# A softmax-times-V kernel: the first bank's normalisation of the last head in a pass placed behind its last transposed copy, that head's exponentials taken row by row, and the last loads cut as 3, 2, 1, 1, 1 rows

## The chip, the cores and the metric

The kernel runs on one core of a Trainium2 chip. The metric is the device time of one execution in microseconds. The kernel before took 1064.57 us (median of 3 runs, 1064.5 to 1064.79). Times in traces are counted from the start of the profiled span, which is some 2 us shorter than the time of the same run.

## The reference

```python
# scores: 8 x 12 x 1024 x 1024 float32, v: 8 x 12 x 1024 x 64 float32
scores_max = np.max(scores, axis=-1, keepdims=True)
attn = np.exp(scores - scores_max)
attn = attn / (np.sum(attn, axis=-1, keepdims=True) + 1e-8)
return np.matmul(attn, v).astype(np.float32)
```

There are 96 heads. The scores alone are 403 MB, read once, so this is a kernel of transfers.

## The kernel before

One pass of a hardware loop works off four heads (k = 0 to 3); there are 24 passes. A head has 8 "rows" (tiles of 128 x 1024). A row goes through these stations: a load by DMA; ScalarE's exponential into fp16; eight transposes on TensorE into a PSUM tile `psT`; VectorE's copy of that into `pt`; eight products with V on TensorE, two rows later in program order. A column of ones beside V gives the sum of the exponentials. After the product of row 3 the first PSUM bank of an odd head is complete, after row 7 the second; `normalise` takes the reciprocal of the sums and multiplies (one reciprocal, two products on VectorE for each bank). No maximum is subtracted.

```python
    def finish(u):                      # the products of one row
        ...
        for c in range(C):
            nc.tensor.matmul(out=bank[:, g * M : (g + 1) * M],
                lhsT=pt[:, c * P : (c + 1) * P], rhs=st["vones"][:, c, 0:M], ...)
        if k % 2 == 1:
            if g == G - 1:
                normalise(k, st, b, b + 1)          # b: bank 0 or 1
        elif r == R - 1:
            normalise(k, st, 0, R // G)
        ...
    # in last(n0), behind the last pass but one: the loads of the very last head, in parts of rows
                load(AHEAD - 1, BH - 1, (2,))
                store(n0, AHEAD - T)
                load(AHEAD - 1, BH - 1, (2, 2, 1, 1), 2)
        ...
    def heads(n0):
        for k in range(AHEAD):
            for r in range(R):
                if r % EB == 0:                      # EB = 2 rows an exponential
                    p_nat = take(p_bufs)
                    rows = 1 if k == AHEAD - 1 and r == R - EB else EB
                    for g in range(0, EB, rows):
                        nc.scalar.activation(...)
                for c in range(C):
                    nc.tensor.transpose(...)
                pt = take(pt_bufs)
                nc.vector.tensor_copy(out=pt[:], in_=psT[:])
                ...
                if len(pending) > LAG:               # LAG = 2
                    finish(pending.pop(0))
```

(Cuts are marked by dots.)

The softmax here doesn't subtract the row's maximum and nothing guards it: scores larger than these inputs give would overflow.

## Time and profile before

| | before |
|---|---|
| time, median of 3 runs | 1064.57 us |
| profiled span | 1062.5 us |
| bytes moved | 453 MB |
| last row of scores landed | 1052.02 us |
| last copy on VectorE starts | 1055.87 us |
| VectorE's last product ends | 1058.37 us |
| last store landed | 1060.67 us |

The prediction below shows the slices and the tail. From the page's list of queues and its table of costly groups, only these lines are added (queue: packets, MB, share of the time of 16 engines; group: line, engine, operation, count, busy us, mean ns, idle before):

```profile
q1 hardware_dynamic: 25056, 453.00, 99.3%
...
L253 ACT ACTIVATE p_nat<-s_nat 128x2048 f16<-128x2048 f32 (+1 forms) x408 | 704.9, 1800 | 219.3 <-DMA s_nat<-in_scores_dram 192.2
```

The queue is full for 99.3% of the span, and the busiest compute engine spends most of its idle time waiting for loaded scores. As long as a change to the engines doesn't move the loads, it can only show after the last byte has landed.

### The profile page before, as it was taken

What the parts mean: (1) busy time and instruction counts of PE and PEld (TensorE: products, weight loads), DVE (VectorE), ACT (ScalarE), POOL (GpSimd) and SP (SyncE); (2) the same over time, 40 slices, a digit from 0 to 9 for tenths busy, and PEclk for the clock granted to TensorE, in tenths of its full rate; (3) what the DMA queues carried; (4) which work ended last, traced back from release to release, by engine and by line L of the source; (5) the groups of instructions that cost most, each with busy time, mean ns of one, the idle gap of its engine ahead of it and who ended that gap; (6) DMA issues with size and microseconds to landing.
All of it is one profiled execution on the core that took longest, in us unless ns stands there. A gap on an engine that the chain in (4) does not pass through costs nothing.

```text
span 1062.5 us, 32878 instructions
## 1 busy us (share of the span) xinstructions
PE 722.2 (68%) x12288; PEld 679.8 (64%) x12288; DVE 682.4 (64%) x1205; ACT 735.7 (69%) x432; POOL 243.5 (23%) x406
## 2 busy tenths in 40 slices
PE   2766766667766767666676666767667676667676
PEld 2765766657666667666676656757666576666675
DVE  1766666757566666666676656766667566666667
ACT  3766776666767668576675866767666677666686
POOL 3123212131121311212112221122121311203113
PEclk9888888888789798887888988888888988887989
DMA  9999999999999999999999999999999999999996
GB/s 398 429 418 434 429 434 434 432 435 432 431 429 432 430 432 435 434 433 432 435 424 434 433 429 435 427 441 433 432 432 427 433 429 435 434 433 433 432 427 257
DMA packets 25060, 453.06 MB, mean 426 GB/s; under 512 B 2784, under 2 KB 2784, under 8 KB 9312
## 3 DMA queue, kind: packets, MB, share of 16 engines
q1 hardware_dynamic: 25056, 453.00, 99.3%
q8 instruction: 4, 0.07, 0.0%
HBM read 436.21 MB, written 25.17 MB: 434 GB/s over the span
## 4 chain that ended last, share of the span: by engine, by line
DMA 61%; PE 15%; PEld 5%; ACT 5%; DVE 4%; issue 3%; POOL 3%; SPq 1%; POOLq 1%; ACTq 0%; PEldq 0%
DMA s_nat<-in_scores_dram 61%; PE psT L265 8%; PE psO L144 6%; ACT p_nat L253 5%; DVE pt L271 4%; PEld L265 3%; POOL vones L210 3%; PEld L144 2%; PE psO_whole L144 2%; SPq L201 1%; SPq L189 0%; POOLq L210 0%; POOLq L227 0%; POOLq L288 0%; POOLq L316 0%
## 5 line engine op out<-in xcount | busy, mean ns | idle before, releaser
L253 ACT ACTIVATE p_nat<-s_nat 128x2048 f16<-128x2048 f32 (+1 forms) x408 | 704.9, 1800 | 219.3 <-DMA s_nat<-in_scores_dram 192.2
L265 PE MATMUL psT<-order,p_nat 128*128 128x128 f16 x6144 | 565.0, 247 | 262.6 <-ACT p_nat L253 261.7
L271 DVE COPY pt<-psT 128x1024 f16<-128x1024 f16 x768 | 519.5, 690 | 348.4 <-PE L144 126.7
L265 PEld LDWEIGHTS <-p_nat 128*128 128x128 f16 x6144 | 448.6, 124 | 284.2 <-ACT p_nat L253 281.8
L210 POOL CAST vones<-v_sb 32x512 f16<-32x512 f32 x400 | 242.8, 607 | 815.9 <-PE L265 315.9
L144 PEld LDWEIGHTS <-pt 128*128 128x128 f16 x6144 | 303.9, 107 | 92.9 <-DVE pt L271 89.2
L144 PE MATMUL psO<-vones,pt 128*128 128x65 f16 x3072 | 183.2, 202 | 59.9 <-DVE pt L271 59.6
L144 PE MATMUL psO_whole<-vones,pt 128*128 128x65 f16 x3072 | 189.3, 209 | 12.3 <-DVE pt L271 11.9
L253 ACT ACT_TABLE_LOAD x24 | 30.8, 1283 | 98.5 <-DMA s_nat<-in_scores_dram 81.7
L128 DVE TENSOR_TENSOR out_sb<-psO,recip 64x256 f32<-64x256 f32 x192 | 81.2, 423 | 6.0
L128 DVE TENSOR_TENSOR out_sb<-psO_whole,recip 64x512 f32<-64x512 f32 x96 | 66.0, 688 | 3.1
L123 DVE RECIPROCAL recip<-psO 128x4 f32<-128x4 f32 x96 | 17.0, 177 | 17.2 <-PE psO L144 17.2
L123 DVE RECIPROCAL recip<-psO_whole 128x8 f32<-128x8 f32 x48 | 9.5, 198 | 0.0
L71 DVE MEMSET vones<- 128x16 f16 x4 | 0.2, 72 | 0.8 <-PEq L305 0.8
L62 DVE CAST order<-ident 128x128 f16<-128x128 f32 x1 | 0.2, 227 | 0.4 <-POOL ident masks.py:199 0.4
masks.py:199 POOL TENSOR_SCALAR_AFFINE_SELECT ident<-ident 128x128 f32<-128x128 f32 x1 | 0.3, 292 | 0.1
masks.py:197 POOL MEMSET ident<- 128x128 f32 x1 | 0.2, 204 | 0.3 <-POOLq L305 0.3
L305 POOL MEMSET const-float32-0.0<- 128x1 f32 x1 | 0.1, 98 | 0.3 <-issue 0.3
L305 POOL MEMSET const-bfloat16-1.0<- 128x1 bf16 x1 | 0.1, 100 | 0.0
L305 POOL MEMSET const-uint8-127<- 128x1 uint8 x1 | 0.1, 100 | 0.0
L305 POOL MEMSET const-float32-1.0<- 128x1 f32 x1 | 0.1, 98 | 0.0
## 6 DMA issues: line engine op xcount, KB each, us to landing
s_nat<-in_scores_dram SPq DMA_DIRECT2D x96, 4096.0 KB, 32.2
v_sb<-in_v_dram SPq DMA_DIRECT2D x24, 1024.0 KB, 18.4
out_dram<-out_sb SPq DMA_DIRECT2D x47, 512.0 KB, 27.6
s_nat<-in_scores_dram SPq DMA_DIRECT2D x2, 2048.0 KB, 33.4
s_nat<-in_scores_dram SPq DMA_DIRECT2D x3, 1024.0 KB, 27.4
s_nat<-in_scores_dram SPq DMA_DIRECT2D x2, 512.0 KB, 20.7
out_dram<-out_sb SPq DMA_DIRECT2D x2, 256.0 KB, 2.0
```

Of the source, the lines that this page charges most:

```text
L62: nc.vector.tensor_copy(out=order16[:].rearrange("p (t j) -> p t j", t=T), in_=ident32[:].rearrange("p (j t) -> p t j", t=T),)
L71: nc.vector.memset(vo[:, :, D : D + 2], 1.0)
L123: nc.vector.reciprocal(out=recip, in_=psO[:, :, :, D : D + 1])
L128: nc.vector.tensor_tensor(out=rows.rearrange("j (b g) d -> j b g d", g=G), in0=psO[part, :, :, 0:D], in1=recip[part].to_broadcast([W, last ...
L144: nc.tensor.matmul(out=bank[:, g * M : (g + 1) * M], lhsT=pt[:, c * P : (c + 1) * P], rhs=st["vones"][:, c, 0:M], start=(c == 0), stop=(c ...
L201: nc.sync.dma_start(out=v_sb[:].rearrange("x h s l d -> x (h s l d)"), in_=rows[bass.ds(n // AHEAD, 1)].rearrange("o x y -> (o x) y"),)
L210: nc.gpsimd.tensor_copy(out=vones_bufs[k][s * Q : (s + 1) * Q, :, 0:D].rearrange("i (h l) d -> i h l d", l=L), in_=v_sb[k * Q : (k + 1) * ...
L253: nc.scalar.activation(out=p_nat[:, g : g + rows, :].rearrange("p r (x v) -> p x r v", v=Q * L), in_=s_bufs[k][:, r + g : r + g + rows, :] ...
L265: nc.tensor.transpose(out=psT[:, c * P : (c + 1) * P], in_=p_row[:, c // L, c % L, :], identity=order16[:],)
L271: nc.vector.tensor_copy(out=pt[:], in_=psT[:])
L305: nc = _bacc.Bacc("TRN2", target_bir_lowering=False, num_devices=1)
```

## The change

The intent: the first bank's reciprocal and products of the last head stand on VectorE in front of the last copy, on which everything after it depends. They are ordered behind that copy, where VectorE otherwise waits for the last products. And the last head comes in smaller parts behind a first one of three rows, with an exponential for each single row, so that ScalarE need not wait for a pair. The order on VectorE and the single-row exponentials (from row 2 on) apply to the last head (k = 3) of every pass, the parts of the loads to the very last head alone.

```diff
-    def normalise(k, st, first, last):
+    def normalise(k, st, first, last, behind=None):
...
-        nc.vector.reciprocal(out=recip, in_=psO[:, :, :, D : D + 1])
+        inverse = nc.vector.reciprocal(out=recip, in_=psO[:, :, :, D : D + 1])
+        if behind is not None:
+            after(inverse, behind)
...
-            if g == G - 1:
+            if g == G - 1 and (b > 0 or k < AHEAD - 1):
                 normalise(k, st, b, b + 1)
...
-                load(AHEAD - 1, BH - 1, (2,))
+                load(AHEAD - 1, BH - 1, (3,))
                 store(n0, AHEAD - T)
-                load(AHEAD - 1, BH - 1, (2, 2, 1, 1), 2)
+                load(AHEAD - 1, BH - 1, (2, 1, 1, 1), 3)
...
-                    rows = 1 if k == AHEAD - 1 and r == R - EB else EB
+                    rows = 1 if k == AHEAD - 1 and r > 0 else EB
...
-                nc.vector.tensor_copy(out=pt[:], in_=psT[:])
+                copy = nc.vector.tensor_copy(out=pt[:], in_=psT[:])
+                if k == AHEAD - 1 and r == R - 1:
+                    normalise(k, st, 0, 1, copy)
```

## The prediction

> **What bounds the kernel now.** I read the page's slices first, then the last 40 us engine by engine in order of time, then single semaphore updates.
>
> The 40 slices of the page:
>
> ```profile
> DMA  9999999999999999999999999999999999999996
> GB/s 398 429 418 434 429 434 434 432 435 432 431 429 432 430 432 435 434 433 432 435 424 434 433 429 435 427 441 433 432 432 427 433 429 435 434 433 433 432 427 257
> ```
>
> For 39 slices the DMA engines are full at about 430 GB/s; only the last slice (26.6 us wide) is not. The change leaves the bytes (453 MB) alone. What it does in the first 23 passes lies beside a full transfer queue (loads take some 32 us from issue to landing, so three are always queued), so I count it as zero, and only the tail can pay.
>
> VectorE in order of time, from 1049.2 us to the end (start, length, operation, idle before it):
>
> ```profile
> 1049.26 0.69 DVE L271 COPY pt<-psT 128x1024 f16<-128x1024 f16 x1 [0.21 <-PE L144]
> 1049.87 0.20 DVE L123 RECIPROCAL recip<-psO_whole 128x8 f32<-128x8 f32 x1
> 1050.10 1.41 DVE L128 TENSOR_TENSOR out_sb<-psO_whole,recip 64x512 f32<-64x512 f32 x2
> 1051.54 2.48 DVE L271 COPY pt<-psT 128x1024 f16<-128x1024 f16 x4
> 1053.94 0.18 DVE L123 RECIPROCAL recip<-psO 128x4 f32<-128x4 f32 x1
> 1054.24 0.69 DVE L271 COPY pt<-psT 128x1024 f16<-128x1024 f16 x1
> 1054.96 0.88 DVE L128 TENSOR_TENSOR out_sb<-psO,recip 64x256 f32<-64x256 f32 x2
> 1055.87 0.69 DVE L271 COPY pt<-psT 128x1024 f16<-128x1024 f16 x1
> 1057.28 0.18 DVE L123 RECIPROCAL recip<-psO 128x4 f32<-128x4 f32 x1 [0.72 <-PE psO L144]
> 1057.49 0.88 DVE L128 TENSOR_TENSOR out_sb<-psO,recip 64x256 f32<-64x256 f32 x2
> ```
>
> Counted back from the end: the copy at 1055.87 is row 7 of the last head, 1054.24 row 6, the four at 1051.54 rows 2 to 5, 1049.26 row 1. Reciprocal and products at 1053.94 to 1055.84 normalise the first bank (rows 0 to 3); nothing needs them until the final store, yet they stand in front of the last copy, on which the last product on TensorE and all after it depend. After that copy VectorE idles 0.72 us.
>
> It looks as if VectorE, busy without a break, were the bound. It is not, quite. TensorE and VectorE in order of time while the first head of this pass is worked off (one fence each):
>
> ```profile
> 1028.57 0.61 PE L265 MATMUL psT<-order,p_nat 128*128 128x128 f16 x8
> 1029.28 0.62 PE L265 MATMUL psT<-order,p_nat 128*128 128x128 f16 x8
> 1029.99 0.61 PE L265 MATMUL psT<-order,p_nat 128*128 128x128 f16 x8
> ```
>
> ```profile
> 1029.73 0.69 DVE L271 COPY pt<-psT 128x1024 f16<-128x1024 f16 x1 [0.27 <-PE L144]
> 1030.69 0.69 DVE L271 COPY pt<-psT 128x1024 f16<-128x1024 f16 x1 [0.27 <-PE L144]
> 1031.65 0.69 DVE L271 COPY pt<-psT 128x1024 f16<-128x1024 f16 x1 [0.27 <-PE psO_whole L144]
> ```
>
> The transposes of rows 5, 6, 7 start 0.71 us apart, their copies 0.96 us apart, each after 0.27 us of idle VectorE, the last one over a microsecond after its transposes seem done. The trace records every semaphore update, and there the answer is: TensorE's semaphore rises by one for each of the 32 instructions of a row (8 weight loads and 8 matmuls for the transposes, as many for the product), one every 0.030 us, so 0.96 us a row, and each of these copies starts within 0.01 us of the update that completes its own transposes. In the tail these updates run without a break from before 1049.27 (row 1's transposes counted) to 1051.64, pause until 1051.88, and run on: row 5 at 1053.29, row 6 at 1054.24, row 7 at 1055.20. Row 6's copy (1054.24) waits for that; row 7's (1055.87) does not, it is 0.67 us late because of the first bank's products.
>
> ScalarE in the same stretch:
>
> ```profile
> 1047.23 1.92 ACT L253 ACTIVATE p_nat<-s_nat 128x2048 f16<-128x2048 f32 x1 [0.67 <-PE L144]
> 1049.64 3.81 ACT L253 ACTIVATE p_nat<-s_nat 128x2048 f16<-128x2048 f32 x3 [0.49 <-PE L265]
> ```
>
> Its two waits are put down to TensorE, but the loads' semaphores show rows 2 and 3 landing at 1047.13, rows 4 and 5 at 1049.54, row 6 at 1050.77, row 7 at 1052.02: it waits for data. The exponentials of rows 4 and 5 end at 1051.56, their transposes start at 1051.61, and that is the pause in the updates.
>
> [...] the last store here is issued from SyncE, and takes 2.05 us from issue at 1058.62 to landing at 1060.67. Nothing in the change shortens that.
>
> **The change, part by part.** Nothing is removed; one normalisation moves, ScalarE gets two more instructions a pass, the last loads are cut otherwise.
>
> *Loads 3,2,1,1,1.* A row of 0.5 MB takes 1.2 us (1049.54, 1050.77, 1052.02). By that step rows 0 to 2 land at 1043.38 + 1.2 = 1044.6, then the store, rows 3 and 4 at 1048.35; rows 5, 6, 7 stay at 1049.54, 1050.77, 1052.02. Total and last landing are the same.
>
> *Single-row exponentials.* A single row takes 1.04 us alone and 0.95 from start to start, against 1.80 for a back-to-back pair: 0.1 us more for a pair, twice a pass, on an engine busy 69%. In the tail row 2 ends near 1047.6, row 3 at 1049.5, row 4 at 1050.45 (1.1 us sooner than now), row 5 at 1051.4, row 6 at 1052.35, row 7 at 1053.3 (now 1053.45). So TensorE no longer pauses for row 4. Counting 0.03 us an instruction on from 1049.27 without the pause, in the changed kernel's own order, 192 instructions bring row 7's transposes to 1049.27 + 5.76 = 1055.03: 0.17 us sooner.
>
> *The moved normalisation.* VectorE's order also changes nearby: row 2's copy now stands before the two large products of the head before. From 1050.07: row 2 waits for its transposes at 1050.23 and ends at 1050.92; large products to 1052.36; row 3 to 1053.08; rows 4, 5 and 6 at 0.60 us steps to 1053.69, 1054.28 and 1054.89 (row 6's transposes are counted at 1054.07); row 7 can start at 1054.81, so its transposes decide: 1055.04 to 1055.73, against 1055.87 to 1056.56 now. The first bank then takes reciprocal and products, 1055.65 to 1056.75. The last product on TensorE is counted 16 instructions after row 6's at 1055.99, at 1056.47 (or 0.69 us after the copy, as now: 1056.42), inside that time, so the 0.72 us wait vanishes and VectorE goes on: second bank 1056.78 to 1057.88, against 1058.37 now. The store follows each half as now. **Sum: 0.49 us**, of which 0.17 from the pause and some 0.32 from the move. 1064.57 - 0.49 = 1064.08.
>
> **The rivals.**
> 1. VectorE's instructions are the bound. Then taking 1.13 us of first-bank work (with its gap) from before the last copy brings that copy forward by all of it, and with the first bank filling the idle 0.72 us the end comes 0.8 us sooner: 1063.8. For it: no idle over 0.2 us before 1056.56. Against: rows 6 and 7 are ready by the count only at 1054.07 and 1055.03.
> 2. The extra 0.27 us returns. Rows 6 and 7 now follow a copy directly, with the two-wait form of instruction that shows 0.27 us of idle elsewhere. If that form itself cost 0.27 us, row 7 would end near 1056.2 and nothing would be gained: 1064.5. Against: the same form without idle at row 6 of the second head (start 1038.70, the count at 1038.71).
> 3. Last landing or TensorE's final product takes over: row 7 lands at 1052.02 and is needed near 1054.5, about 1.2 us spare after its exponential; the product has 0.3 us spare. A slip there costs tenths: 1064.3.
> 4. GpSimd's four casts after the last product run to 1060.02 now, the store's landing to 1060.67; both move earlier, so the casts stay hidden. No effect.
> 5. The first 23 passes gain or lose through earlier stores: with DMA at 99.3% I expect nothing. Were I wrong by 0.05 us a pass, that would be 1.2 us.
>
> **Range and chances.** The mechanisms span 0.0 to 0.8 us; the three runs of before spread over 0.3 us, and another session may shift the level by some tenths. So 1064.1, from 1063.4 to 1064.7. Two per cent is 21 us, more than the whole unfilled tail after the last landing (10.5 us): within 2% at 0.98, 0.01 on either side for a slow execution.
>
> **What would show it.** In the changed profile the last copy starts at the count of its transposes, near 1055.0 relative to the same loads, with no idle of 0.7 us behind it; two reciprocals and four products follow each other to VectorE's end, near 1057.9; no TensorE pause before row 4. Wrong, if the last copy starts well before the count would allow (rival 1), if 0.27 us gaps stand before rows 6 and 7 with the count long done (rival 2), or if the slices before the last change their GB/s (rival 5).

(0.49 us is 0.17 from the pause and some 0.32 from the move, all from the times and the 0.030 us steps read above.)

## The result, and the profile after

The changed kernel took **1064.06 us** (median of 6 runs, 1063.72 to 1064.94); the kernel before took 1064.59 us in the same rounds (6 runs, 1064.39 to 1064.93). A ratio here is the mean time of one kernel's fast runs over the mean of the other's of the same rounds, so not quite the ratio of the medians: it is 0.9996, with a 95% interval from 0.9984 to 1.0009. By the times alone this is "the same"; that there is a real half microsecond must come from the traces, and from the fact that the difference of the medians was 0.53, 0.66 and 0.47 us in three sets of rounds.

The slices of the page after:

```profile
DMA  9999999999999999999999999999999999999996
GB/s 397 430 417 434 428 434 434 432 435 428 434 432 432 427 433 435 434 434 427 433 429 435 428 433 435 426 441 431 431 434 429 430 428 438 434 434 432 426 432 260
```

The first 39 slices are as full as before: the first 23 passes gained and lost nothing.

VectorE of the changed kernel in order of time (start, length, operation, idle before it):

```profile
1049.42 0.69 DVE L273 COPY pt<-psT 128x1024 f16<-128x1024 f16 x1 [0.21 <-PE L146]
1050.03 0.20 DVE L123 RECIPROCAL recip<-psO_whole 128x8 f32<-128x8 f32 x1
1050.38 0.69 DVE L273 COPY pt<-psT 128x1024 f16<-128x1024 f16 x1 [0.15 <-PE L146]
1051.11 1.41 DVE L130 TENSOR_TENSOR out_sb<-psO_whole,recip 64x512 f32<-64x512 f32 x2
1052.54 2.48 DVE L273 COPY pt<-psT 128x1024 f16<-128x1024 f16 x4
1055.18 0.69 DVE L273 COPY pt<-psT 128x1024 f16<-128x1024 f16 x1 [0.16 <-PE L146]
1055.79 0.17 DVE L123 RECIPROCAL recip<-psO 128x4 f32<-128x4 f32 x1
1056.00 0.88 DVE L130 TENSOR_TENSOR out_sb<-psO,recip 64x256 f32<-64x256 f32 x2
1056.91 0.18 DVE L123 RECIPROCAL recip<-psO 128x4 f32<-128x4 f32 x1
1057.12 0.88 DVE L130 TENSOR_TENSOR out_sb<-psO,recip 64x256 f32<-64x256 f32 x2
```

Row 7's copy starts at 1055.18, the trace's record of TensorE's semaphore completes that row's transposes at 1055.16, and the idle of 0.16 us in front of it is that wait. Behind it two reciprocals and four products follow without the idle of 0.72 us of before. Row 2's copy now stands before the two large products, as the prediction said.

ScalarE of the changed kernel:

```profile
1048.45 4.86 ACT L255 ACTIVATE p_nat<-s_nat 128x1024 f16<-128x1024 f32 x5 [0.93 <-PE L267]
```

Five single rows in one unbroken run, the last one ending at 1053.30 (before 1053.45). Rows 3 and 4 landed at 1048.37; here too the wait is put down to TensorE, where the landing was last.

TensorE's transposes and VectorE's copies while the second half of this pass's first head is worked off (one fence each), as in the prediction:

```profile
1029.15 0.61 PE L267 MATMUL psT<-order,p_nat 128*128 128x128 f16 x8
...
1029.85 0.61 PE L267 MATMUL psT<-order,p_nat 128*128 128x128 f16 x8
...
1030.56 0.61 PE L267 MATMUL psT<-order,p_nat 128*128 128x128 f16 x8
```

```profile
1030.01 0.69 DVE L273 COPY pt<-psT 128x1024 f16<-128x1024 f16 x1 [0.27 <-PE L267]
1030.97 0.69 DVE L273 COPY pt<-psT 128x1024 f16<-128x1024 f16 x1 [0.27 <-PE L267]
1031.93 0.69 DVE L273 COPY pt<-psT 128x1024 f16<-128x1024 f16 x1 [0.27 <-PE psO_whole L146]
```

The same 0.71 against 0.96 us as before. In the tail the updates of the semaphore run without any pause from row 1 to the last product.

| us from the span's start | before | after | after, as predicted |
|---|---|---|---|
| rows 0-1 (before), 0-2 (after) landed | 1043.38 | 1044.55 | 1044.6 |
| row 7 landed | 1052.02 | 1052.02 | 1052.02 |
| row 1's transposes counted | 1049.24 | 1049.40 | 1049.27 |
| row 7's transposes counted | 1055.17 | 1055.16 | 1055.03 |
| last copy starts | 1055.87 | 1055.18 | 1055.04 |
| VectorE's end | 1058.37 | 1058.00 | 1057.88 |
| last store landed | 1060.67 | 1060.30 | |

("Counted" is the time of the semaphore's update by the last of a row's 16 instructions. The prediction reads these times one update, 0.03 us, too late, and so does its column here: the pass has 1024 updates, and in the kernel before the pause begins behind update 864, which is the last one before row 4's transposes. Counted rightly, the copies that wait start some 0.02 us behind their update.)

So the trace shows 0.37 us gained where 0.49 was predicted, and the difference is there already at row 1: the whole stream of counts runs 0.16 us later. What delays it lies before the tail. This was the open question for the experiments, beside the proof of the counting itself.

### The profile page after: what moved, and what is told of

Its sections match the earlier page's. It is cut to its first block, busy times and chain, and to the rows that moved or that the text cites. A ratio compares the mean times of both kernels' runs of the same rounds, so it can differ in the third digit from the quotient of the medians.

```text
span 1062.3 us, 33094 instructions
## 1 busy us (share of the span) xinstructions
PE 722.0 (68%) x12288; PEld 676.5 (64%) x12288; DVE 679.9 (64%) x1205; ACT 740.1 (70%) x480; POOL 243.5 (23%) x406
## 4 chain that ended last, share of the span: by engine, by line
DMA 62%; PE 12%; PEld 6%; DVE 5%; ACT 5%; issue 3%; POOL 3%; SPq 1%; POOLq 1%; ACTq 0%; DVEq 0%; PEldq 0%
DMA s_nat<-in_scores_dram 62%; PE psT L267 7%; DVE pt L273 5%; ACT p_nat L255 5%; PE psO L146 3%; POOL vones L212 3%; PEld L267 3%; PEld L146 3%; PE psO_whole L146 1%; SPq L203 1%; SPq L191 0%; POOLq L212 0%; POOLq L229 0%; POOLq L293 0%; POOLq L321 0%
## 5 line engine op out<-in xcount | busy, mean ns | idle before, releaser
L146 PE MATMUL psO<-vones,pt 128*128 128x65 f16 x3072 | 177.5, 202 | 41.4 <-DVE pt L273 39.8
```

Of the source, the lines that this page charges most:

```text
L146: nc.tensor.matmul(out=bank[:, g * M : (g + 1) * M], lhsT=pt[:, c * P : (c + 1) * P], rhs=st["vones"][:, c, 0:M], start=(c == 0), stop=(c ...
```

## The experiments

Eleven runs were made in three calls, all with correct results, the first call on chip 0 and the other two on chip 7. Within a call they share the runs of the kernel before: 1064.76 us in the first call, 1065.36 in the second, 1064.61 in the third (medians of 9 runs each).

To compare profiles whose loads fall a little differently, one anchor is used: the start of the first exponential of the second head of the last pass (1030.06 us in the kernel before), which starts when that head has landed. (The expectations name it the third head; that is a slip, k = 1 is the second.) "Half clock" is the stretch with a granted clock of 0.50 between 1022 and 1030 us. A "window" is 3.413 us: in the clock records of both traces, before and after, every stretch of half or full clock is a whole number of windows long, except the last, which ends with the trace (half clock: one or two windows, full clock: two or more), and in each trace all begin on one grid of that step, to 0.003 us. The grid runs through all passes of some 43.7 us, 12.8 windows each, without being set anew by one. How it lies to the last pass is called the phase.

| run | half clock, us | anchor to that head's first copy | to the last copy | to VectorE's end | median time | ratio to before |
|---|---|---|---|---|---|---|
| before | 3.4 | 2.67 | 25.81 | 28.31 | 1064.57 | 1 |
| after | 6.8 | 2.87 | 25.16 | 27.98 | 1064.06 | 0.9996 |
| e_again | 6.8 | 2.87 | 25.16 | 27.97 | 1064.10 | 0.9997 |
| e_move | 6.8 | 2.89 | 25.42 | 28.23 | 1064.40 | 0.9996 |
| e_split | 6.8 | 2.87 | 26.02 | 28.51 | 1064.56 | 0.9999 |
| e_oldloads | 3.4 | 2.67 | 24.96 | 27.78 | 1063.95 | 0.9993 |
| e_warm | none | 2.67 | 24.97 | 27.78 | 1063.89 | 0.9989 |
| e_again2 | 3.4 | 2.67 | 24.96 | 27.78 | 1064.14 | 0.9996 |
| e_oldloads2 | 3.4 | 2.67 | 24.96 | 27.78 | 1064.06 | 0.9993 |
| e_both | none | 2.67 | 25.09 | 27.91 | 1064.23 | 0.9995 |
| e_warmbefore | none | 2.67 | 26.10 | 28.60 | 1065.28 | 1.0005 |

(e_dummy and e_unroll, which change the count itself, stand below.) The 95% interval of each of these ratios is about 0.0013 to either side and contains 1. The times can't rank kernels that are tenths of a microsecond apart; the columns of the traces can, since they repeat to 0.02 us.

### The changed kernel again

No edit.

> The changed kernel once more, unaltered, to have it beside the parts in the same rounds. All theories: about 0.5 us under the kernel before in the median; in the trace the last copy starts within 0.02 us of the count of its transposes, near 3.2 us after row 7 has landed, and VectorE ends some 6.0 us after that landing (before: 6.35).

Measured: 1064.10 us (1063.81 to 1064.93, 5 runs). Row 7 landed at 1052.15, VectorE ended 6.00 us later (5.98 in the first profile). The result repeats, and so does the late stream.

### The normalisation moved alone

```diff
 against the changed kernel
-                load(AHEAD - 1, BH - 1, (3,))
+                load(AHEAD - 1, BH - 1, (2,))
-                load(AHEAD - 1, BH - 1, (2, 1, 1, 1), 3)
+                load(AHEAD - 1, BH - 1, (2, 2, 1, 1), 2)
-                    rows = 1 if k == AHEAD - 1 and r > 0 else EB
+                    rows = 1 if k == AHEAD - 1 and r == R - EB else EB
```

> Only the first bank's normalisation is moved behind the last copy; loads and exponentials as before. My theory (TensorE's completion count releases the last copies; the move alone is worth the difference seen): the count of row 7's transposes stays 3.2 us after the landing of row 7, no idle before the second bank, VectorE ends 6.0 us after that landing, like the full change: 0.3 to 0.5 us faster than before. Rival (VectorE's own instructions are the bound): the last copy comes 1.1 us sooner, VectorE ends 5.5 us after the landing. Rival (the cut of loads and exponentials gives a third of the gain, 0.17 us): ends 6.15 after the landing.

Measured: 1064.40 us (1064.03 to 1064.58). VectorE:

```profile
1051.64 2.50 DVE L273 COPY pt<-psT 128x1024 f16<-128x1024 f16 x4
1054.40 0.69 DVE L273 COPY pt<-psT 128x1024 f16<-128x1024 f16 x1 [0.27 <-PE psT L267]
1055.36 0.69 DVE L273 COPY pt<-psT 128x1024 f16<-128x1024 f16 x1 [0.27 <-PE L146]
```

With the bank's work out of the way, rows 6 and 7 do not move up to the copies before them. They stand 0.96 us apart with 0.27 us idle before each, which is the count's pace. VectorE ended 6.06 us after row 7 had landed, against 6.35 in the kernel before. That lies between the theory's 6.0 and the 6.15 of the rival that gives a third of the gain to the loads and exponentials, and can't decide between them, since the landings themselves moved: row 7's is 22.17 us behind the anchor here, 21.96 in the kernel before. The count's pause before row 4, which the move leaves in place, was 0.25 us. The section on why the prediction was right takes this up: the rival's third was right.

### The loads and exponentials alone

```diff
 against the changed kernel: as in the kernel before again
-            if g == G - 1 and (b > 0 or k < AHEAD - 1):
+            if g == G - 1:
                 normalise(k, st, b, b + 1)
...
-                if k == AHEAD - 1 and r == R - 1:
-                    normalise(k, st, 0, 1, copy)
```

> Only the loads 3,2,1,1,1 and the single-row exponentials; the first bank's normalisation stays in front of the last copy. My theory: TensorE's count no longer pauses for row 4, so row 7's transposes are counted 0.15 us sooner (3.0 us after the landing), but VectorE is then the later one, because row 2's copy now waits in front of the two large products: last copy near 4.1 us after the landing (before 3.85), VectorE's end 6.6 us after it, so 0.0 to 0.3 us slower than before. Rival (the data's arrival limits the tail): 0.2 us faster than before.

Measured: 1064.56 us (1064.47 to 1065.84). VectorE's last stretch:

```profile
1055.10 0.88 DVE L128 TENSOR_TENSOR out_sb<-psO,recip 64x256 f32<-64x256 f32 x2
1056.01 0.69 DVE L271 COPY pt<-psT 128x1024 f16<-128x1024 f16 x1
1057.41 0.18 DVE L123 RECIPROCAL recip<-psO 128x4 f32<-128x4 f32 x1 [0.72 <-PE psO L144]
```

The bank's products stand in front of the last copy and the idle of 0.72 us is back. Row 7's copy starts 4.05 us after the row landed, VectorE ends 6.54 after: no gain at all from this half by itself. (The profiled run is this kernel's slowest; its last store took unusually long, to 1062.28. The tail on VectorE is not touched by that.)

### The changed kernel with the old parts of the loads

```diff
-                load(AHEAD - 1, BH - 1, (3,))
+                load(AHEAD - 1, BH - 1, (2,))
-                load(AHEAD - 1, BH - 1, (2, 1, 1, 1), 3)
+                load(AHEAD - 1, BH - 1, (2, 2, 1, 1), 2)
```

> The full change, but the last head's loads in parts of 2,2,2,1,1 as before. My theory: the cut of the loads is worth nothing, because the single-row exponentials alone take away the pause for row 4 (its data lands at the same time as before and its exponential ends 0.9 us sooner): VectorE's end 6.0 us after the last landing, time as for the full change within 0.1 us. Rival (the loads' cut matters): 0.15 us or more later.

Measured: 1063.95 us (1063.74 to 1064.15). The last copy starts 3.00 us after row 7 landed and VectorE ends 5.82 after, sooner than the full change in its first two profiles (5.98 and 6.00). It looked as if the new parts of the loads cost 0.2 us. The anchor says otherwise: the 0.20 us are there at the second head's first copy, before any of those loads matter.

### Two more instructions a row on TensorE

```diff
         for c in range(C):
             nc.tensor.matmul(...)
+        for x in range(2):
+            nc.tensor.matmul(
+                out=bank[0:32, 300 + x : 301 + x], lhsT=pt[:, 0:32],
+                rhs=st["vones"][:, 0, 0:1], start=True, stop=True,
+            )
```

The two products have one column each and write a part of the bank that nothing reads. With their weight loads they make 36 instructions of 32.

> The changed kernel with two more tiny matmuls per row on TensorE (32 columns of weights, one column moving, written to an unused column of the product's bank): 36 instructions a row in place of 32. Theory (the count, one instruction every 0.030 us, paces the last pass): copies in the last pass start 1.08 us apart in place of 0.96, and over the some 27 rows of the unbroken count the last copy and the end come 3.2 us later (2.6 to 3.6). Rival (TensorE's work itself or VectorE paces it): TensorE's rows take 0.71 us, with the tiny pairs at most 0.85, so the copies stay 0.96 apart and the time changes by less than 0.5 us.

Measured: 1068.22 us (1068.06 to 1069.04), ratio 1.0030, interval 1.0015 to 1.0045. VectorE at the turn from the third head of the last pass to the fourth (two rows of the one, the first of the other):

```profile
1049.75 0.69 DVE L281 COPY pt<-psT 128x1024 f16<-128x1024 f16 x1 [0.39 <-PE psT L275]
1050.83 0.69 DVE L281 COPY pt<-psT 128x1024 f16<-128x1024 f16 x1 [0.39 <-PE L146]
1051.91 0.69 DVE L281 COPY pt<-psT 128x1024 f16<-128x1024 f16 x1 [0.39 <-PE L146]
```

The copies are 1.08 us apart instead of 0.96: 36 x 0.030 us. VectorE idles 0.39 us before each. Four instructions with next to no work in them cost 0.12 us a row, and the kernel is 2.9 us slower than before and some 3.4 us slower than the changed kernel (taking 0.5 us for its gain). By the trace VectorE ends 9.07 us after row 7 has landed, where the changed kernel took 5.98: 3.1 us belong to the tail. The landing itself (1053.29) is some 0.9 us later than in any other run of the loop; why is open. The count sets the pace of the last pass.

### The loop written out

```diff
-    with tc.For_i(0, BH, AHEAD, iteration_sync="reg_based") as n0:
+    for n0 in range(0, BH, AHEAD):
 ... and the branches on n0 decided in Python
```

In this form only 888 of TensorE's 24,576 instructions increment a semaphore.

> The changed kernel with the loop over passes written out: the same instructions, but outside a loop the framework gives an increment to only 888 of TensorE's 24,576 instructions in place of all. Theory: copies in the last pass follow TensorE's work at 0.71 to 0.95 us a row (ScalarE's pace) in place of 0.96, the backlog is gone, the last copy starts within 2.7 us of the last landing in place of 3.2, VectorE ends 4.6 to 5.2 us after it in place of 6.0. Rival (TensorE really needs 0.96 us a row): the same 6.0 us. The whole time may go either way: 1.2 us less in the tail, but some 2 MB of instructions to fetch (up to 5 us at 430 GB/s): 1062.5 to 1068.

Measured: 1080.23 us (1079.94 to 1080.68), ratio 1.0141. The last copy starts 5.04 us after the last landing and VectorE ends 7.84 after. The expectation was missed, and it is no clean test: the order of the instructions came out differently too. Row 7's transposes and the copy of them (TensorE and VectorE):

```profile
1072.03 0.61 PE L261 MATMUL psT<-order,p_nat 128*128 128x128 f16 x8
```

```profile
1072.68 0.69 DVE L267 COPY pt<-psT 128x1024 f16<-128x1024 f16 x1 [0.91 <-PE psT L261]
```

The copy starts 0.04 us after its transposes seem done (1072.64). In the changed kernel they seem done at 1054.77 and the copy starts at 1055.18, 0.41 us later. So without the stream of increments the lag of the count is gone, as the theory says. The pace is gone too, which the rival of this run (TensorE really needs 0.96 us) excludes: in the second head of the last pass the copies of rows 3 to 6 start at 1051.83, 1052.53, 1053.23 and 1053.94, 0.70 us apart, each 0.04 us after its own transposes seem done. But here TensorE starts row 7's transposes late: row 7's exponential ended at 1068.89, and in TensorE's own order products of earlier rows, which wait for their copies, stand in front. The other 15.6 us come before the tail: the last row lands at 1067.64. The profile shows 1.73 MB more moved (454.78 MB), all of it on the queues of instructions (1.78 MB against 0.05), which at some 430 GB/s is an estimate of 4 us; the rest is left open.

### Idle products that keep the clock up

```diff
         while pending:
             finish(pending.pop(0))
+        for x in range(40):
+            warm = nc.tensor.matmul(
+                out=psO_whole[:, 0, 300:428], lhsT=order16[:], rhs=order16[:],
+                start=True, stop=True,
+            )
+            after(warm, latest[0])          # behind the last product of the pass
         last(n0)
```

> The changed kernel with 40 idle matmuls on constants behind the last product of every pass, so that TensorE doesn't idle 2.9 us before the next pass. Theory (the change lets TensorE's clock fall earlier, and this takes 0.16 us of its gain back): granted clock near 1.0 instead of 0.5 between 1024 and 1029 us, the first head's copies at 0.96 us a row, row 1 of the last head counted 0.1 to 0.25 us sooner relative to the landings, row 7 near 3.0 us after the last landing, end 0.15 us sooner than the full change. Rival (the later start of the count has another cause): no difference beyond 0.05 us in the trace.

Measured: 1063.89 us (1063.87 to 1064.59), ratio 0.9989. The granted clock is 1.00 from 1022 to 1029 us, where the changed kernel has 0.50, the anchor's distance 2.67 instead of 2.87, the last copy at 24.97 instead of 25.16. With the half clock taken away, the 0.2 us is gone.

### The changed kernel a third time

No edit. In the traces the grid of windows runs on through the passes. If chance decides how it lies to the last pass, a further profile may show the shorter stretch.

> The changed kernel unaltered, for a third set of rounds beside the others of this call: 1063.7 to 1064.9 us, 0.3 to 0.6 us below the kernel before. [...] a stretch of one window (about 3.4 us) would give 2.67 us from the third head's first exponential to its first copy, a stretch of two (6.8 us) 2.87. If the stretch is two windows in all three profiles of this kernel, it is tied to the longer idle of TensorE before the last pass and not to chance.

Measured: 1064.14 us (1063.89 to 1064.86). The view of stretches has for each stretch its length, the busy time of each engine with the number of instructions, then TensorE's granted clock, the DMA share and GB/s. The changed kernel in its first profile:

```profile
1027.00:1028.00 1.00, 1.00 (x16) 1.00 (x15) 0.40 (x2) 1.00 (x2) 0.00 (x0) 0.50 0.84 348
1028.00:1029.00 1.00, 1.00 (x15) 1.00 (x13) 0.45 (x1) 0.93 (x1) 0.00 (x0) 0.51 1.30 549
```

and the same kernel in this run:

```profile
1027.00:1028.00 1.00, 1.00 (x23) 1.00 (x22) 0.60 (x2) 1.00 (x2) 0.00 (x0) 0.94 0.95 393
1028.00:1029.00 1.00, 1.00 (x28) 1.00 (x26) 0.73 (x2) 0.94 (x1) 0.00 (x0) 1.00 1.24 524
```

The clock is full again 1.9 us sooner; TensorE gets through 28 matmuls in a microsecond instead of 15. The distances are 2.67, 24.96 and 27.78: 0.20 us better than in the first two profiles of the same code, and equal to those of the run with old loads. The half clock lasted 3.4 us here and 6.8 there. It is the length of the half clock, not the change and not the parts of the loads; the two profiles fit a length that follows the phase. The first transposes start at 1023.58 us in both. In the first profile a window began before them, at 1022.16, had TensorE busy for 1.99 of 3.41 us, and a second one at half clock followed; here one began behind that start, at 1023.68, was busy throughout, and the full clock followed. No run set the phase on purpose. This kernel alone doesn't exclude the chip as a cause (e_again ran on chip 0, this run on chip 7), but e_oldloads, on chip 0, had the single window as well.

### The old loads again

No edit to the run with old loads.

> The changed kernel with the old parts (2,2,2,1,1 rows) again: is its lead over the changed kernel real? Clock theory: 0.1 to 0.2 us below the changed kernel of the same rounds, with one window of half clock (3.4 us) and a distance of 2.67 us from the third head's first exponential to its first copy. Rival (chance of the phase): two windows and 2.87 us this time, and the same time as the changed kernel within 0.05 us.

Measured: 1064.06 us (1063.81 to 1064.65), one window of half clock, distances 2.67, 24.96 and 27.78, as in its first run. But its lead over the changed kernel does not hold up: e_again2, beside it, has the same three distances, and the medians are 0.08 us apart. Its earlier lead was that of a shorter half clock.

### Old loads and idle products together

The two edits above in one kernel.

> The changed kernel with the old parts of the last head (2,2,2,1,1 rows), keeping the single-row exponentials and the moved normalisation, and with 40 idle matmuls behind each pass that keep TensorE's clock up: the candidate to beat both. Clock theory (the half clock between 1022 and 1029 us put the count of the last pass 0.16 to 0.20 us behind in the changed kernel; where the clock is full in time the first row of the third head is released by the landing of that head instead, its copy 2.67 us behind the head's first exponential): that distance is 2.67 us (2.87 in the changed kernel), the last copy starts 24.96 us behind that exponential (25.16), VectorE ends 0.45 to 0.6 us before the kernel before of the same phase, and the time is that of the run with old loads alone, 1063.7 to 1064.1 us on an equal chip, since both cures remove the same 0.2 us. Rival (the idle matmuls save something of their own, as their ratio of 0.9989 suggests): 0.3 to 0.5 us below the run with old loads in the same rounds.

Measured: 1064.23 us (1064.16 to 1064.26), so neither the expected time nor a version that beats the others: the last copy at 25.09 instead of 24.96. Row 7 landed at 1052.34 in this run, 22.19 us behind the anchor against 21.96 in e_oldloads, and its exponential started only 0.61 us after that, because rows 4 and 5 land together and ScalarE then has a run of four rows to work off. It ended at 1053.99, its transposes started at 1054.09. In e_warm the row landed as late (22.19) and its exponential started 0.24 us after; nothing was lost. Here the new parts of the loads show what they are good for: not time, but room. In the changed kernel the last exponential ends 0.86 us before its transposes start (1053.30 to 1054.16), with the old loads 0.32 us (1053.65 to 1053.97), and 0.10 in e_both.

### The kernel before with idle products

```diff
 against the kernel before: the 40 products of e_warm, nothing else
```

> The kernel before with the same 40 idle matmuls behind each pass and nothing else. Clock theory: in the kernel before the half clock ended in time (1027.6 us), the third head's first copy already starts 2.67 us behind its exponential, so nothing is gained: last copy and VectorE's end as in the kernel before (25.81 and 28.31 us behind that exponential), time the same within 0.2 us. Rival (the idle matmuls bring about 0.9 us by themselves, the part of the ratio 0.9989 that the tail does not explain): about 0.7 us faster than the kernel before.

Measured: 1065.28 us (1064.66 to 1065.60). The rival, that the idle products save 0.7 us of their own, falls. The clock theory's distance at the head's first copy holds (2.67), but the tail came out 0.29 us later than in the kernel before (26.10 and 28.60), and the time is 0.67 us longer, which I had not expected. Row 7's landing is again 22.19 us behind the anchor against 21.96, and its exponential ended at 1053.89 against 1053.45. The tail's 0.29 us can be followed in the trace: rows 4 and 5 landed 19.77 us behind the anchor instead of 19.48, their exponential started at 19.87 instead of 19.58, and the count's pause before row 4 grew from 0.18 to 0.46 us. So it is the landings that were late. That the last landing fell at 22.19 in all three kernels with idle products might be their doing; but e_again2, e_move and e_dummy, without them, have 22.15, 22.17 and 22.19. This stays open. As a cure the idle products are not worth having.

## Why the prediction was right

The time (1064.06 measured, 1064.1 predicted), the range and the class held. Step by step:

- **Only the tail pays.** Right. The slices are the same, the last row lands at 1052.02 in both, and the difference of VectorE's ends (0.37 us) is that of the last landings of the store (1060.67 - 1060.30).
- **The loads and exponentials.** Right to 0.05 us for the landings (1044.55, 1048.37) and to 0.1 for the exponentials (rows 2 to 7 end at 1047.52, 1049.51, 1050.46, 1051.41, 1052.36, 1053.30). The pause of the count is gone.
- **The count as the pace.** Right. It is the step on which rival 1 stood or fell: the copies keep 0.96 us in e_move, and 1.08 us in e_dummy with four more instructions a row. VectorE looked busy without a break and still was not the bound.
- **Counting on from 1049.27.** This is the step that failed in the profile of the change: the text took the starting point of the count over from the profile before, and it was 0.16 us later (1049.40 for 1049.24). All that follows was 0.12 to 0.16 us late with it, the last copy (1055.18 for 1055.04) and VectorE's end (1058.00 for 1057.88). In its place the runs showed that the start of the stream has two values, 0.20 us apart, for the same code. With one window of half clock the second head's first row is released 2.67 us behind the anchor, by its own exponential. With two windows, TensorE is so far behind on the first head that the count of that head's rows holds the second one up, to 2.87: in the changed kernel that copy (1032.89) follows the one before it (1031.93) at the count's 0.96 us, in the kernel before (1032.73 behind 1031.65) it does not.
- **The sum of 0.49 us.** At equal half clock (before and e_again2, both with one window) VectorE ends 28.31 - 27.78 = 0.53 us sooner. So the sum was 0.04 us short, and 0.03 of that is the count read one update too late. The 0.37 of the first profile is the 0.53 less 0.20 for the longer half clock, and 0.04 more because the anchor itself came 0.04 us sooner.
- **0.17 for the pause and 0.32 for the move.** The split is confirmed, with a correction to how it reads. The kernel before counts row 7's transposes at 1055.17. Had its copy started 0.02 us after that, as in e_move, and VectorE ended 2.81 us after the copy's start, as there, the end would have been 1058.00, 0.37 us sooner: an estimate of what the move is worth alone, 0.05 over the prediction. The other 0.16 of the 0.53 us is the pause, predicted at 0.17; read from the count itself it is 0.18 us in the kernel before. Between e_move and the changed kernel lie 28.23 - 27.98 = 0.25 us, but there the pause was longer, because rows 4 and 5 landed 19.76 us behind the anchor instead of 19.48. The loads and exponentials by themselves bring nothing: e_split's 28.51 is, less the 0.20 of the longer half clock, the 28.31 of before. So the two parts are not addends; the second pays only once the first has made the count the bound. In the second part it is the exponentials that pay: with the old loads (e_oldloads) the distances are those of e_again2.
- **Rival 2 (0.27 us of the instruction's form).** It falls: in the changed kernel rows 3 to 6 are copied in one run without a gap, and row 7 after 0.16 us, at its count. Where 0.27 us appears (e_move) the count is due at that moment, and in e_dummy it is 0.39.
- **Rival 3 (landing, last product).** It did not happen in the changed kernel. It did, by a tenth, in e_both, where the last exponential left 0.10 us.
- **Rivals 4 and 5.** Nothing in the slices or in the last store's landing speaks for them.

What remains of the argument rather than of a run: that the half clock's length makes the 0.20 us was shown by e_warm and e_again2, and that it comes in whole windows by the lengths (3.4 and 6.8 us), but the phase was not set on purpose, and the kernel before was seen with one window only. If it too can have two, its tail would be longer by up to 0.2 us in some of its runs, an estimate from the 2.87 and 2.67 us of the changed kernel.

## What to carry to other kernels

Before taking an engine that shows no idle time for the bound, compare the pace of its instructions with that of the semaphore that releases them: here each update of TensorE's semaphore came 0.030 us behind the one before, even with products of a single column (36 instructions a row put the copies 1.08 us apart, 32 put them 0.96), so this long stream of small ones was paced by their number. When one of two obstacles on the same path is removed, ask which is then next; a part that brings nothing alone may bring a third of the gain on top of the other. And for a difference of tenths of a microsecond, profile the same code more than once: here one kernel had two tails 0.20 us apart.

## What the runs showed of the count and the clock

- The count: an update came 0.030 us behind the one before (the median step from 1030 to 1056 us, in before and in after). Weight loads count as well as matmuls (32 updates for 16 products and transposes), and the lag builds up over a stream of rows (0.96 us a row against the 0.71 at which TensorE starts its transposes; 1.08 with 36 instructions), so that in e_dummy it set the pace of the last pass and made the tail 3.1 us longer.
- The clock: the half-clock stretches of the table were 3.4 or 6.8 us, one window or two (none in the runs with idle products), and the changed kernel had both. Their start does not keep to the program: the stretch began 7.86 us before the anchor in the first profile of the changed kernel and 6.29 in e_again2. The clock fell after windows in which the profile has TensorE busy for 1.32 of 3.41 us (the changed kernel, 1018.75 to 1022.16) or 1.04 (the kernel before, 1020.83 to 1024.24), stayed down after one with 1.99 (1022.16 to 1025.57, all of it transposes at half clock), and rose after ones with 3.01 and 3.41. Counted over all windows of the trace of before: it fell after 67 windows with at most 1.62 us busy, stayed full after 142 with at least 1.58, stayed half after 28 with at most 2.71 and rose after 66 with at least 2.76. So the clock also fell after windows that were not empty.
- A second window of half clock, where the semaphore's count is the bound, cost 0.20 us here. It put the last copy of the pass's first head 0.52 us later (1.91 us behind the anchor in the changed kernel, 1.39 in e_again2), and the wait for the second head's data took all but 0.20 of that back.
